# Two transformer blocks on one core: pacing GpSimd's products, and smaller matmul groups in five places

## The chip, the cores and the metric

The kernel runs on one core of a Trainium2 chip. The metric is the device time of one execution in microseconds (us). Three timed runs of the kernel before gave 1594.9, 1595.97 and 1597.15 us (median 1595.97).

A core has five engines, each with an instruction queue of its own that it works off in order: PE (TensorE, matrix products, results into PSUM banks), DVE (VectorE), ACT (ScalarE), POOL (GpSimd, which can't read PSUM) and SP (used here to issue the weight DMAs).

## The reference

256 tokens of width 1024 go through two blocks. All operands are float32.

- The first block: root-mean-square norm; a projection to the inputs of four branches and their gates; a short convolution, stick-breaking attention, an RWKV-7 recurrence and a spatial gating unit (`w_causal` times the normalised `v`, plus a bias `b_s` per group and position, times `u`); the gated sum of the branches, a projection, a residual; then a feed-forward part, `(silu(gate) * val) @ w_down`, with a depthwise convolution of three taps over `h @ w_up` (2 x 2816 columns).
- In the recurrence, `decay = exp(-c * sigmoid(w0 + tanh(xw) @ w2))`, with a bias row `w0` of 256 values.
- The second block: 16 memory tokens are put in front; a state-space branch (S5) with complex diagonal states, an mLSTM branch whose input and forget gates are `concat(q, k, v) @ w_if + b_if`, a gated sum; then a product-key retrieval of experts (128 x 128 experts) and a final norm.

## The kernel before, in words

**Weights.** All weights come as tiles of 128x128; eight of them are a unit, one DMA of 512 KB issued by SP. Each unit is split into a rounded part `wh` (ACT, line 339) and the rest `wl` (DVE, line 340), and each product of float32 accuracy is three matmuls (lines 405 to 407: high times high, high times low, low times high), 24 per unit for 256 tokens. `enter` (line 322) loads up to seven units and splits up to three units ahead, and calls `tick`.

**Background generators.** Work beside the stream of units (the recurrence, the attention, the constants of the S5 branch in `_prep`) is written as Python generators. `tick` (line 366) gives a credit of 1.2 per unit and takes one step of each generator as long as credit is left; a step's yield names its price. `step` and `behind` (lines 348 to 360) put what a step traces on PE, ACT and DVE behind the split and the matmul of some units before, with `tc.issue_after(ins)`: it queues the instructions traced within the block on `ins`'s own engine behind `ins`, in issue order only. On POOL there is no such edge. Apart from these edges and the data, the order of each engine's queue is written by the compiler's planner, which goes by when it expects an instruction's operands.

**The feed-forward loop** (lines 1871 to 1949) has 22 tiles of 128 columns. `up(i)` takes two units (gate and value), 48 matmuls, the convolution on ACT and DVE, silu on ACT, and the gating product `u[:, 0] * u[:, 1]`, which is on POOL for the first 19 tiles (line 1892). The split of a gated tile (ACT's cast, line 429, and DVE's rest, line 430) is traced one tile later, and `down(i - 2)`, 24 matmuls, two tiles later. So three units, 72 matmuls, belong to a tile.

**`_prep`** runs beside that loop from tile 1 on. `paced` (line 559) makes a complex product of 128x512 values as six POOL instructions in four steps (lines 563 to 566). There are eight such products: three of them build the input matrices `bx`, one `c0`, four the output matrices `cx`; then line 583 negates 2048 columns. Beside the last four, eight groups of transposes (line 591) and four groups of small products (line 599) run on PE. Last, eight folds: POOL expands three small matrices (`expand`, lines 490 to 492, called in 635 and 636), PE multiplies each with `w_if` (lines 639 to 641), ACT copies the result.

**Other lines that the change touches.** Lines 1446 to 1451: `tanh(xw) @ w2` on PE, with the bias `w0` added by a product of a row of ones with the row `w0`. Lines 1765 to 1773: eight products of the spatial gating unit into halves of a PSUM bank (64 rows each), each followed by a product of a row of ones with the bias row `sgb`. Lines 839 to 845: the gates of the mLSTM, 16 products that write 8 rows of PSUM each, accumulated in one place. Lines 1276 to 1278: the residual is brought into the four output accumulators by products with the identity, 16 of 128x128. Lines 448 to 457: `rstd` sums squares over the channels with a matrix of ones; it is called after the second projection tile (line 1430), and `K.normed` and the shifts follow from there. Lines 1349 to 1357 issue the first DMAs.

## Time and profile before

| | |
|---|---|
| time, median of three runs | 1595.97 us |
| the profiled execution | 1592.86 us |
| its span | 1591.0 us |
| mean granted TensorE clock | 0.987 |
| busy, share of the span | PE 96%, DVE 72%, ACT 52%, POOL 15% |
| feed-forward loop on PE | 289.3 to 536.1 us |
| read from HBM | 253.23 MB |

The span runs from the first to the last instruction. Busy is the time in which an engine works on an instruction; a busy PE need not run at full clock. In the rows further down, a line of a timeline gives start, duration, engine, line of the kernel and operation, the tile written and those read, the shape and the count of merged instructions; in brackets stands the idle time before it and what ended it. A product of two float32 operands appears as two records, one of the rounded kind as one. A table of stretches gives start and end, length, then for each engine its busy time and its count of instructions, the granted clock as a share of 2.4 GHz, and the DMA engines' share.

### The profile page before, as it was taken

How to read it: one execution, taken by the hardware profiler on the slowest of the kernel's cores; microseconds unless marked ns; L12 is line 12 of the kernel's file. 1: busy time of each engine (PE TensorE's matmuls, PEld its weight loads, DVE VectorE, ACT ScalarE, POOL GpSimd, SP SyncE). 2: the span in 40 equal slices, each digit the busy share in tenths (PEclk: the TensorE clock that was granted, in tenths of full speed). 3: DMA queues.
4: the chain of work that ended last, by engine and by line, in shares of the span. 5: the costliest groups of instructions: out<-in, count | busy, mean ns of one | idle time of the engine just before them, and what ended most of it. 6: DMA issues, size and time to landing. Idle time of an engine off the chain costs nothing.

```text
span 1591.0 us, 29719 instructions
## 1 busy us (share of the span) xinstructions
PE 1535.2 (96%) x11661; PEld 1425.3 (90%) x11661; DVE 1146.4 (72%) x2164; ACT 832.5 (52%) x1439; POOL 237.4 (15%) x254
## 2 busy tenths in 40 slices
PE   7999999987599999999999999999999999999998
PEld 7999899987599997889999999999999888888886
DVE  7765467865477788668899888788999566566664
ACT  7654345744345556555554554544444555555554
POOL 2000000275613002000100431112222000000000
PEclk9999999998899999999999999999999999999999
DMA  7543245544255553245545555555545556556563
GB/s 258 160 136 119 80 133 173 193 146 136 91 174 163 171 166 111 93 134 167 190 159 183 177 158 186 161 161 170 159 160 165 185 194 196 191 195 192 193 197 107
DMA packets 80717, 257.94 MB, mean 162 GB/s; under 512 B 17345, under 2 KB 18881, under 8 KB 80322
## 3 DMA queue, kind: packets, MB, share of 16 engines
q1 hardware_dynamic: 69200, 247.32, 48.3%
q10 hardware_dynamic: 11378, 8.73, 1.9%
q8 instruction: 92, 1.51, 0.4%
q14 instruction: 47, 0.39, 0.1%
HBM read 253.23 MB, written 2.13 MB: 161 GB/s over the span
## 4 chain that ended last, share of the span: by engine, by line
PE 84%; POOL 7%; DVE 6%; ACT 1%; issue 1%; DMA 1%; SPq 0%; ACTq 0%; POOLq 0%; DVEq 0%
PE acc L1297 22%; PE U L405 7%; PE U L407 6%; PE U L406 6%; POOL s L564 4%; PE g L405 3%; PE g L406 3%; PE g L407 3%; DVE wl L340 2%; PE pG L1177 2%; PE u L405 2%; PE u L406 1%; PE u L407 1%; PE q L406 1%; PE q L405 1%; PE q L407 1%
## 5 line engine op out<-in xcount | busy, mean ns | idle before, releaser
L340 DVE TENSOR_TENSOR wl<-wr,wh 128x1024 fp32r<-128x1024 f32 (+1 forms) x469 | 587.4, 1255 | 196.0 <-ACT wh L339 193.1
L339 ACT CAST wh<-wr 128x1024 fp32r<-128x1024 f32 (+1 forms) x469 | 490.6, 1048 | 393.7 <-PE U L406 156.8
L1297 PE MATMUL acc<-wh,wring 128*128 128x512 f32 x1024 | 315.5, 389 | 0.0
L405 PE MATMUL U<-hh,wh 128*128 128x256 f32 x1024 | 292.5, 286 | 0.0
L407 PE MATMUL U<-hh,wl 128*128 128x256 f32 x1024 | 288.1, 281 | 1.5 <-DVE wl L340 1.4
L406 PE MATMUL U<-hl,wh 128*128 128x256 f32 x1024 | 288.3, 282 | 0.0
L1297 PEld LDWEIGHTS acc<-wh,wring 128*128 128x128 f32 x1024 | 192.2, 188 | 40.0
L1297 PE MATMUL acc<-wl,wring 128*128 128x512 f32 x512 | 199.2, 389 | 0.0
L407 PEld LDWEIGHTS U<-hh,wl 128*128 128x128 f32 x1024 | 193.9, 189 | 1.9 <-DVE wl L340 1.9
L405 PEld LDWEIGHTS U<-hh,wh 128*128 128x128 f32 x1024 | 193.4, 189 | 0.0
L406 PEld LDWEIGHTS U<-hl,wh 128*128 128x128 f32 x1024 | 192.5, 188 | 0.0
L1288 ACT ACTIVATE wring<-act 128x256 fp32r<-128x256 f32 x128 | 53.3, 418 | 152.2 <-PE acc L1297 148.7
L1297 PEld LDWEIGHTS acc<-wl,wring 128*128 128x128 f32 x512 | 96.1, 188 | 19.8
L405 PE MATMUL u<-hh,wh 128*128 128x256 f32 x320 | 92.9, 292 | 12.3 <-ACT wh L339 11.6
L1289 DVE SCALAR_TENSOR_TENSOR wring<-act,wring 128x256 fp32r<-128x256 f32 x128 | 54.6, 427 | 60.5 <-PE acc L1297 57.3
L407 PE MATMUL u<-hh,wl 128*128 128x256 f32 x320 | 92.0, 288 | 3.2 <-DVE wl L340 3.2
L406 PE MATMUL u<-hl,wh 128*128 128x256 f32 x320 | 91.4, 287 | 0.0
L1258 POOL TENSOR_TENSOR act<-act,ga 128x16 f32<-128x16 f32 (+31 forms) x77 | 56.5, 733 | 212.4 <-ACT ga L1257 192.3
L444 POOL TENSOR_TENSOR sq<-sq,sq 128x256 f32<-128x256 f32 x18 | 16.0, 888 | 415.4 <-ACT sq L440 415.1
L405 PEld LDWEIGHTS u<-hh,wh 128*128 128x128 f32 x320 | 62.3, 195 | 13.2 <-ACT wh L339 12.0
L405 PE MATMUL g<-hh,wh 128*128 128x256 f32 x256 | 73.8, 288 | 0.0
L406 PE MATMUL g<-hl,wh 128*128 128x256 f32 x256 | 72.0, 281 | 0.0
(643 smaller groups left out, 3411.6 us busy)
## 6 DMA issues: line engine op xcount, KB each, us to landing
wr<-in_W SPq DMA_DIRECT2D x211, 512.0 KB, 3.9
wr<-in_U SPq DMA_DIRECT2D x128, 512.0 KB, 3.9
wr<-in_V SPq DMA_DIRECT2D x128, 512.0 KB, 4.3
s<-in_s5p ACTq DMA_DIRECT2D x1, 1056.0 KB, 6.0
tkc<-in_keysT ACTq DMA_DIRECT2D x1, 1024.0 KB, 6.4
wsA<-in_cst ACTq DMA_DIRECT2D x1, 804.0 KB, 5.2
wsA<-in_rows ACTq DMA_DIRECT2D x1, 640.0 KB, 7.0
s<-s ACTq DMA_DIRECT2D x10, 64.0 KB, 3.0
```

Of the source, the lines that this page charges most:

```text
L339: a = nc.scalar.copy(hi[:, q], raw[:, q])
L340: b = nc.vector.tensor_tensor(lo[:, q], raw[:, q], hi[:, q].bitcast(F32), ALU.subtract)
L405: mm(out, wh, ah, start=first, stop=False)
L406: mm(out, wh, al, start=False, stop=False)
L407: self.last = mm(out, wl, ah, start=False, stop=last).ins
L444: self.nc.gpsimd.tensor_tensor(self.part[0], self.part[0], s, ALU.add)
L564: g.tensor_tensor(*z)
L1177: mm(o, ring[:, q % 2, e // 2, :, e % 2], ring[:, q % 2, 4 + 2 * w + e // 2, :, e % 2], start=w == 0, stop=w == 1)
L1258: g.tensor_tensor(d[:, :n], d[:, :n], a[:, :n], ALU.mult)
L1288: act(hi, w, AF.Copy, scale=1.0 / 16384)
L1289: stt(lo, w, 1.0 / 16384, hi.bitcast(F32), ALU.mult, ALU.subtract)
L1297: mm(acc[t][c], w[:, q], v[:, 4 * c:4 * c + 4].rearrange("p a b -> p (a b)"), start=False, stop=i == NE - 1 and len(vs) == 1, skip_group_c ...
```

## The change

- `up` remembers its gating product (`K.pace`); the block products of `_prep` (six per complex product, the two negations) and the expansions for the folds are traced within `issue_after` of it.
- Each fold's three products are made of halves: rows 0 to 63 and 64 to 127 of the matrices, which are block-diagonal, go into rows 0 to 63 and 64 to 127 of PSUM.
- The 16 products of the mLSTM's gates go in turn to rows 0, 32 and 64 of the bank, that is, to three column groups of PE; the three partial sums are added on ACT and DVE.
- The residual's 16 products with the identity become transposes (`is_transpose=True`).
- The biases `w0` and `sgb` are added on DVE; `sgb` is loaded spread over 128 partitions by two DMAs.
- The start: a tile of zeros is set on POOL, 8 matmuls of zeros with 512 columns are traced before the first DMA, and 3, 6 and 3 more between the first four tiles of the first projection. Only the first 8 columns of `cols` come early, unit 1 of the weights comes before the rest of them and before `eye`. `rstd` is called within the third projection tile, on a bank of the other pool, and the norm and the shifts start one tile later.

```diff
-        self.splits, self.last = [], None
+        self.splits, self.last, self.pace = [], None, None
+    def paced(self):
+
+        return ExitStack() if self.pace is None else self.tc.issue_after(self.pace)
-    def lin(self, seg, i0, kt, hi, lo, out):
+    def lin(self, seg, i0, kt, hi, lo, out, between=None):
         for k in range(kt):
+            if between:
+                between(k)
             wh, wl = self.w(seg, i0 + k)
             self.mm3(out, wh, wl, hi(k), lo(k), k == 0, k == kt - 1)
+    def spin(self, n):
+
+        p = self.pm_("spin")
+        for _ in range(n):
+            self.nc.tensor.matmul(p, self.idle[:, :P], self.idle, start=True, stop=True)
-    def rstd(self):
+    def rstd(self, bank=None):
-        ms = self.ps("ms")[:, :T1]
+        ms = (bank or self.ps)("ms")[:, :T1]
...
         for n, z in enumerate(ops):
-            g.tensor_tensor(*z)
+            with K.paced():
+                g.tensor_tensor(*z)
...
-    g.tensor_scalar(nc0, c0[1], -1.0, None, ALU.mult)
+    with K.paced():
+        g.tensor_scalar(nc0, c0[1], -1.0, None, ALU.mult)
...
-        g.tensor_scalar(cx[1], cx[1], -1.0, None, ALU.mult)
+        with K.paced():
+            g.tensor_scalar(cx[1], cx[1], -1.0, None, ALU.mult)
...
     for e in range(8):
-        for i in range(3):
-            expand(tr[i], e, ex[:, i])
+        with K.paced():
+            for i in range(3):
+                expand(tr[i], e, ex[:, i])
         yield 0.3
         pf = K.ps("pf")
-        mm(pf[:, 0:8], ex[:, 0], wif[:, e], start=True, stop=False)
-        mm(pf[:, 0:8], ex[:, 1], wif[:, 8 + e], start=False, stop=True)
-        mm(pf[:, 8:16], ex[:, 2], wif[:, 16 + e], start=True, stop=True)
+        for i in range(3):
+            for q in (slice(0, 64), slice(64, 128)):
+                mm(pf[q, i // 2 * 8:i // 2 * 8 + 8], ex[q, i, q], wif[q, 8 * i + e], start=i != 1, stop=i != 0)
...
         pg = K.pm_("pg")
-        for e in range(8):
-            mm(pg[:8, :T2], fold[:, 0, e], xc[:, e], start=e == 0, stop=False)
-        for e in range(8):
-            mm(pg[:8, :T2], fold[:, 1, e], xp[:, e, 3:], start=False, stop=e == 7)
+
+        for i in range(16):
+            q = slice(32 * (i % 3), 32 * (i % 3) + 8)
+            mm(pg[q, :T2], fold[:, i // 8, i % 8], (xc[:, i % 8], xp[:, i % 8, 3:])[i // 8], start=i < 3, stop=i > 12)
         act(ga[:8], pg[:8, :T2], AF.Identity, bias=mp[:8, 480:481])
+        for i, z in ((1, gl), (2, gB)):
+            scopy(z[:8], pg[32 * i:32 * i + 8, :T2])
+            tt(ga[:8], ga[:8], z[:8], ALU.add)
...
-            mm(o, xr[:, k, t * P:(t + 1) * P], K.ident, start=k % 4 == 0, stop=False, skip_group_check=True)
+            mm(o, xr[:, k, t * P:(t + 1) * P], K.ident, start=k % 4 == 0, stop=False, is_transpose=True, skip_group_check=True)
...
+    K.idle = K.misc.tile([P, 512], F16, name="idle", tag="ix")
+    nc.gpsimd.memset(K.idle, 0.0)
     act(K.misc.tile([P, 2], F32, name="warm"), eps, AF.Copy)
+    K.spin(8)
     for a, b in ((0, 1), (1, 2), (2, 4), (4, 8)):
         nc.sync.dma_start(xr[:, a:b], I["xT"][:, a:b])
         if a == 0:
-            nc.sync.dma_start(cols, I["cols"])
+            nc.sync.dma_start(cols[:, :8], I["cols"][:, :8])
             K.load(1)
         if a == 1:
             K.piece(1)
+    K.load(2)
+    nc.sync.dma_start(cols[:, 8:], I["cols"][:, 8:])
     nc.sync.dma_start(eye2, I["eye"])
...
-    sgb = C2.a(512)
+
+    sgb = C2.a(2, P)
     with K.behind():
-        nc.scalar.dma_start(sgb[0:1], I["sgb"])
+        for e in range(2):
+            nc.scalar.dma_start(sgb[64 * e:64 * e + 64],
+                                I["sgb"].rearrange("o (c e t) -> o c e t", e=2, t=P)[:, :, e].to_broadcast([64, 2, P]))
...
-        K.lin("rw", j * 8, 8, h0, l0, p[:, :T1])
+        def between(k):
+            nonlocal rs
+            if j == 0 and 0 < k < 4:
+                K.spin((3, 6, 3)[k - 1])
+            if j == 2 and k == 4:
+                rs = K.rstd(K.pm_)
+
+        K.lin("rw", j * 8, 8, h0, l0, p[:, :T1], between)
         wait.append((n, p[:, :T1]))
-        if j == 1:
-            rs = K.rstd()
+        if j == 2:
             nrm = K.start(K.normed(xr, COL["mix_norm_g"], rs, hi1, lo1, T1))
-        if j:
+        if j > 1:
...
-            mm(o, txw[:64, c * P:(c + 1) * P], small[:64, 0:256], start=True, stop=False)
-            mm(o, K.ones[0:1, :], row("rw_w0", 1), start=False, stop=True)
-        act(sg, pL, AF.Tanh, scale=0.5)
+            mm(o, txw[:64, c * P:(c + 1) * P], small[:64, 0:256], start=True, stop=True)
+        tt(sg, pL.rearrange("p (a b) -> p a b", a=2), _bc(row("rw_w0"), 1, 2), ALU.add)
+        act(sg, sg, AF.Tanh, scale=0.5)
...
-                    mm(o, gv[:, t, g * 64:g * 64 + 64], gw[:, g], start=True, stop=False)
-                    mm(o, K.ones[0:1, 0:64], sgb[0:1, g * P:(g + 1) * P], start=False, stop=True)
-        tt(gu, gu, pmx.rearrange("p (a b) -> p a b", a=2), ALU.mult)
+                    mm(o, gv[:, t, g * 64:g * 64 + 64], gw[:, g], start=True, stop=True)
+        four = lambda z: z.rearrange("p c (t b) -> p c t b", t=2)
+        mixed = four(gv)
+        tt(mixed, four(pmx.rearrange("p (a b) -> p a b", a=2)), _bc(sgb, 2, 2), ALU.add)
+        tt(gu, gu, gv, ALU.mult)
...
-        (nc.gpsimd.tensor_tensor if i < NFF - 3 else tt)(u[:, 0], u[:, 0], u[:, 1], ALU.mult)
+        prod = (nc.gpsimd.tensor_tensor if i < NFF - 3 else tt)(u[:, 0], u[:, 0], u[:, 1], ALU.mult)
+        K.pace = prod.ins if i < NFF - 3 else None
```

## Rows read from the trace of the kernel before

**Rows 1.** The page: busy us, share and count of an engine; the chain by engine.
```profile
PE 1535.2 (96%) x11661; PEld 1425.3 (90%) x11661; DVE 1146.4 (72%) x2164; ACT 832.5 (52%) x1439; POOL 237.4 (15%) x254
...
PE 84%; POOL 7%; DVE 6%; ACT 1%; issue 1%; DMA 1%; SPq 0%; ACTq 0%; POOLq 0%; DVEq 0%
```

**Rows 2.** Stretches of the feed-forward loop: PE, PEld, DVE, ACT, POOL, clock, DMA.
```profile
328.00:443.30 115.30, 84.91 (x658) 83.10 (x657) 60.80 (x75) 42.65 (x70) 78.64 (x58) 0.87 0.39 125
455.60:504.50 48.90, 48.90 (x419) 48.90 (x417) 38.62 (x93) 24.73 (x47) 18.38 (x30) 1.00 0.59 180
```

**Rows 3.** Timeline of POOL, 327 to 425 us.
```profile
327.73 1.07 POOL L564 TENSOR_TENSOR s<-s,s 128x512 f32<-128x512 f32 x1
...
335.75 3.90 POOL L564 TENSOR_TENSOR s<-s,s 128x512 f32<-128x512 f32 x2
...
343.11 0.72 POOL L1892 TENSOR_TENSOR ffn<-ffn 128x256 f32<-128x256 f32 x1
...
419.44 5.36 POOL L583 TENSOR_SCALAR s<-s 128x2048 f32<-128x2048 f32 x1
```

**Rows 4.** Waits, 328 to 443 us: us in total, times, longest us.
```profile
ACT ffnr L429 <- POOL ffn L1892: 56.6, 8, 16.6
```

**Rows 5.** Lines 564 and 340 (455 to 504, 328 to 343 us): count, ns min/median/max.
```profile
L564 POOL TENSOR_TENSOR s<-s,s x28: 1043/1051/2035, 323.3 to 417.0; 128x512 f32<-128x512 f32 x28
L564 POOL TENSOR_TENSOR s<-s x20: 1042/1284/2250, 328.9 to 418.1; 128x512 f32<-128x512 f32 x20
...
L340 DVE TENSOR_TENSOR wl<-wr,wh x16: 1209/1222/1737, 460.8 to 502.1; 128x1024 fp32r<-128x1024 f32 x16
...
L340 DVE TENSOR_TENSOR wl<-wr,wh x4: 1214/1874/2299, 328.8 to 336.7; 128x1024 fp32r<-128x1024 f32 x4
```

**Rows 6.** Timeline of PE, 181 to 193 us (attention's values, spatial gating).
```profile
180.98 0.66 PE L1733 MATMUL po<-wsE 128*64 128x256 f32 x4
181.46 0.40 PE L1734 MATMUL po<-wsE 128*64 128x128 f32 x4
...
184.33 0.43 PE L1771 MATMUL pmx<-wsF 128*64 128x128 f32 x2
184.69 0.43 PE L1772 MATMUL pmx<-wsF,eye 1*64 1x128 f32 x2
...
188.29 0.68 PE L1772 MATMUL pmx<-wsF,eye 1*64 1x128 f32 x2
...
191.37 0.58 PE L405 MATMUL br<-ysplit,wh 128*128 128x256 f32 x1
```

**Rows 7.** The stretch 190 to 200 us, columns as in rows 2.
```profile
190.00:200.00 10.00, 10.00 (x61) 8.59 (x61) 5.74 (x9) 2.03 (x3) 0.00 (x0) 0.74 0.05 17
```

**Rows 8.** Timeline of PE at 1232 us (residual) and 237 us (transposes).
```profile
1232.24 3.73 PE L1278 MATMUL acc<-eye,X 128*128 128x128 f32 x32
1235.73 0.47 PE L1297 MATMUL acc<-wh,wring 128*128 128x512 f32 x1
...
237.15 0.60 PE L1676 MATMUL pyt<-eye,wsC 128*128 128x128 f32 x4
237.50 0.36 PE L405 MATMUL g<-hh,wh 128*128 128x256 f32 x1
```

**Rows 9.** Timeline of PE, 624 to 633 us (the mLSTM's gates).
```profile
624.78 3.83 PE L841 MATMUL pg<-ml,s 128*8 128x272 f32 x16
...
632.21 0.38 PE L405 MATMUL g<-hi,wh 128*128 128x256 f32 x1
```

**Rows 10.** Timeline of PE, 41 to 43 us (the decay's bias).
```profile
41.09 0.69 PE L1449 MATMUL pL<-wsA,eye 1*128 1x256 f32 x2
41.72 0.70 PE L1448 MATMUL pL<-wsA,wsB 64*128 64x256 f32 x2
```

**Rows 11.** Timeline of PE, 476 to 477 us (one fold).
```profile
476.40 0.28 PE L639 MATMUL pf<-ml 128*128 128x8 f32 x2
...
476.76 0.37 PE L641 MATMUL pf<-ml 128*128 128x8 f32 x2
```

**Rows 12.** Timeline of PE, 15 to 17 us (the first norm).
```profile
15.97 0.70 PE L453 MATMUL ms<-sq,eye 128*128 128x256 f32 x2 [1.51 <-POOL sq L444]
```

More of the change, by code (lines that the diff above doesn't have):

```diff
@@ L1423, in shift @@
         stt(zp[:, n], zz[:, n, 0:T1], col("rw_mu", n), zp[:, n], ALU.mult, ALU.add)
-    wait = []
+    wait, rs = [], None
     for j, n in enumerate(RW_ORDER):
         p = K.ps("z")
-        K.lin("rw", j * 8, 8, h0, l0, p[:, :T1])
+        def between(k):
[5 more added lines that the diff above has]
+        K.lin("rw", j * 8, 8, h0, l0, p[:, :T1], between)
         wait.append((n, p[:, :T1]))
-        if j == 1:
-            rs = K.rstd()
+        if j == 2:
             nrm = K.start(K.normed(xr, COL["mix_norm_g"], rs, hi1, lo1, T1))
-        if j:
+        if j > 1:
             for w in wait:
```

## The prediction, made before the result was known

> **What bounds the kernel now.** I read the page's busy shares and chain first, then the stretches, then the queue that the worst stretch names. TensorE is busy for 96% of the span, and the chain that ended last runs over it for 84% [rows 1]; but the same row gives 7% to POOL, an engine that is busy for 15%. So most of the kernel gains only from less TensorE work, and somewhere POOL holds TensorE up.
>
> The stretches show where. Undisturbed, the feed-forward part issues 419 matmuls in 48.9 us, 0.1167 us each, at full clock. From 328 to 443.3 us it issues 658 in 115.3 us [rows 2]. At 0.1167 us these are 76.8 us, so 38.5 us are lost there, partly as idle time and partly because the granted clock averages 0.87 of 2.4 GHz, that is, it dropped to the 1.2 GHz level between stalls. POOL is busy for 78.6 of those 115.3 us.
>
> POOL's queue gives the cause: ten block products (L564) stand between 327.73 and 343.11, and only then comes the gating product L1892, which itself takes 0.72 us [rows 3]. ACT's cast of the gated tile waits for it, 56.6 us in eight waits, up to 16.6 us [rows 4], and in ACT's in-order queue the weight casts (L339) stand behind that cast. The second batch ends with the 5.36 us of L583 [rows 3].
>
> **The change, part by part.**
>
> *Block products behind gating products.* Nothing is removed: 48 products (28 of one form, 20 of another [rows 5]) now may issue only behind the last gating product traced. How many stand between two gating products? The background generator makes one step per weight unit; six products are four steps, so 1.5 per unit; a tile of the feed-forward loop has three units (two up, one down), so 4.5 products per tile. Alone they take about 1.05 and 1.28 us [rows 5], so 4.5 cost 5.1 us, and with the gating product (0.72 [rows 3]) POOL needs 5.8 us per tile. TensorE needs 72 x 0.1167 = 8.4 us per tile. The gating product is next due one tile later, when its queue is empty again: the 10 to 16 us waits go, and with them the clock's falls. What is late next? POOL and DVE disturb each other: the weight split L340 takes 1.22 us undisturbed and 1.87 in the first bad stretch [rows 5], and a pair of products takes 3.90 instead of 2.1 us beside it [rows 3, 5]. In those 3.90 us fit 2.1 us of products and, at 1.87 apiece, two splits of 1.22: 4.5 us of work, so only some 15% overlaps. Per tile that is 3 x 1.22 + 5.8 = 9.5 us of both, or 8.1 us with this overlap: just under TensorE's 8.4. The upper bound of the loss is no overlap at all (1.1 us per tile); all 48 products take 48 / 4.5 = 10.7 tiles, so 0 to 12 us. I take 2 us, since the 15% come from this very pair of instructions and the weights are split up to three units ahead. The expansions for the folds are paced too: three POOL instructions per unit, each fold needing those traced a unit before, and behind a gating product that ends after the next down unit has begun. Three gating products fall into these eight steps, so 0 to 3 waits of up to 2.5 us; I take 1.5. Gain: 38.5 - 3.5 = 35 us (bounds 38.5 and 38.5 - 12 - 7.5 = 19).
>
> The Trainium skill, "SBUF — State Buffer", section "Who interferes with whom", says that a DVE instruction with two SBUF inputs and a GpSimd instruction that reads SBUF hold a common port exclusively, the second waiting in full. The trace nearly agrees (4.5 us of work in 3.90). By the rule the loss would be the 12 us, and the total 10 us higher; that outcome is the second rival.
>
> *Spatial biases to VectorE.* From 184.33 to 191.37, 7.04 us, eight products of 128x128 alternate with eight of one row; each pair of records takes 0.36 us, and from 188.29 on 0.6 [rows 6], because the clock fell: granted 0.74 in 190 to 200 us [rows 7]. The one-row half goes. Left are 16 records of 128 columns, 0.109 us each by the 32 of [rows 8] (3.49 us), 1.75 us in series; two column halves side by side are cheaper: four records of 256 columns took 0.48 us from 180.98 to 181.46 [rows 6], against 0.87 at the 0.232 us per 272 columns of [rows 9]. I take 1.5 us, gain 5.5 (bounds 5.3 and 6.0). The 18 or so slow matmuls behind it cost about 0.1 us each more than at full clock; if the clock no longer falls (the engine then does 1.5 instead of 7 us of thin work), 1.6 us more; bounds 0 and 1.6, I take 1.6. The replacing DVE additions are off the path: DVE is busy 5.7 of 10 us there [rows 7], and the block that uses the result comes a branch later. The two small DMAs instead of one cost ACT's queue one more issue, in the start.
>
> *Decay bias to VectorE.* Two pairs of one-row records go, 0.63 us each (41.09 to 41.72 [rows 10]): 1.3 us, bounds 1.0 and 1.3. The DVE addition (half the length of the 1.22 us split, so about 0.7 us) delays only the background chain.
>
> *Memory gates in three column groups.* 32 records take 624.78 to 632.21, 7.43 us, in series [rows 9]. Two halves ran 1.8 times as fast as in series in [rows 6]; three groups at best 3 times. Bounds 7.4 and 2.5 us; I take 2.8, near the best, as all are the same shape: gain 4.6. The two copies and two additions it adds are on 8 partitions, some 1.6 us of the chain; that chain starts 4.6 us sooner, which covers them.
>
> *Residual by transposes.* 32 records, 3.49 us [rows 8], become 16; four transposes take 0.35 us (237.15 to 237.50 [rows 8]), so 16 take 1.4: gain 2.1, bounds 1.7 and 2.1.
>
> *Folds by halves.* Six products of half size for three: twelve records instead of six; a pair now takes 0.28 us, three pairs about 0.6 [rows 11]. Halves may overlap and each turn to another shape may cost; between +3 and -3 us over eight folds, I take 0.
>
> *Start: zeros, earlier unit 1, later norm.* TensorE waited 1.51 us for the squares at 15.97 [rows 12]; moving that product 12 matmuls or more back removes the wait. Against it: 20 products of zeros with 512 columns, 0.47 us or less each at full clock [rows 8], double at half: 9.4 us if none were hidden. But the first eight run before data has landed, and the others in gaps where the first matmuls wait for their inputs. What is late next is the weight splits, which ACT and DVE finish at much the same time as before, since ACT issues the constants' DMAs ahead of them and now one more. The norm's scale comes some 1.4 us later, and what waits for it is DVE. Bounds -4 and +2.5; I take +0.5.
>
> Sum: 35 + 5.5 + 1.6 + 1.3 + 4.6 + 2.1 + 0 + 0.5 = 50.6 us. The profiled execution took 1592.86 us (span 1591.0 and 1.86 around it), which gives 1542.3; it lies 3.1 us under the median of the timed runs, 1595.97, from which the same sum gives **1545**. That is my forecast, with a range of its own of 1536 to 1556.
>
> **The rivals.**
> 1. *Port-bound feed-forward.* POOL and DVE take turns without overlap, gating products come late by a few us all the way, and ACT's cast blocks the weight casts again, in small. For it: products of 1.95 us instead of 1.05 [rows 3]. Against: only while a split runs beside them. Price: 10 us more than I took and 6 of late waits: 1561. It decides from 8.4 us of joint work per tile.
> 2. *Only the pacing pays.* Column groups stay serial, the clock falls in spatial mixing all the same, the zeros cost 4: only 35 + 5.3 + 1.3 + 2.1 - 4 = 40 us: 1556.
> 3. *The pacing doesn't spread.* An edge bounds a product only from below; if the planner still puts ten in a row before a gating product, only the TensorE terms stay, 15.6 us: 1580. Against: the edges allow 4 or 5 behind each.
> 4. *Slower.* TensorE is in order and takes 20 steps that POOL feeds (eight groups of transposes, four of kernel products, eight folds). If POOL's products come late at each because they are held behind gating products, TensorE waits 20 times. From 50.6 / 20 = 2.5 us per step the change loses; at 3 us it is 1605. For it: the fold steps, with a gating product between expansion and use. Against: the transposes' inputs are traced five units, 14 us, before.
>
> **How the numbers follow.** Forecast 0.68, rival 1 0.13, rival 2 0.09, rival 3 0.05, rival 4 0.05. The range 1534 to 1564 takes in rivals 1 and 2 and most of the forecast's own; rivals 3 and 4 and some tails are left out, about 0.18. Differences under 0.2%, 3 us, can't be told from none here. Faster is everything but rival 4 and a small share between: faster 0.93, same 0.02, slower 0.05.
>
> **What would show it.** Pacing: POOL's queue with 4 or 5 block products and then a gating product, ACT's wait for the gating product under 10 us in total, granted clock 1.00 from 328 on, and the feed-forward part about 35 us shorter. Splits near 1.9 us throughout and TensorE waiting for them mean rival 1. Spatial mixing: no one-row matmuls and a block of about 1.5 us, clock 1.00 behind it. Gates: 32 records within 3 us. Residual: 16 records in 1.4 us. Start: no wait for the squares, and the fortieth microsecond reached with about as many matmuls. The prediction is wrong if the feed-forward part gains under 19 us, or if TensorE waits for POOL-fed steps.

## The result, and the profile after

After the change the kernel takes 1555.86 us (median of four runs, 1554.12 to 1556.91), against 1595.43 us for the kernel before on the same chip: a ratio of 0.9751, 95% interval 0.9734 to 0.9768. That is 39.6 us, where 50.6 were forecast; in the profiled spans it is 37.1 us (1591.0 and 1553.9). The sign held, and the forecast's own range of 1536 to 1556 us held by 0.14 us; the size was 11 us too large.

The page after, lines that answer to [rows 1]: busy us with share and count, then the chain by engine.

```profile
PE 1523.9 (98%) x11693; PEld 1416.5 (91%) x11693; DVE 1163.0 (75%) x2168; ACT 832.5 (54%) x1441; POOL 250.5 (16%) x255
...
PE 78%; DVE 11%; POOL 4%; issue 2%; ACT 2%; DMA 1%; SPq 0%; ACTq 0%; DVEq 0%; POOLq 0%
```

POOL does a little more than before and stands for 4% of the chain where it stood for 7. To place the gain I took the start of the first matmul of each part in both traces and noted how far ahead the changed kernel was at that point:

| First matmul of | before, us | after, us | ahead, us | gained in the part before it |
|---|---|---|---|---|
| attention's queries (q) | 37.50 | 36.82 | 0.7 | start 0.7 |
| attention's values (v) | 56.58 | 54.47 | 2.1 | decay bias 1.4 |
| output of the mixers (o) | 266.03 | 256.33 | 9.7 | spatial bias and the clock behind it 7.6 |
| feed-forward (u) | 289.32 | 279.62 | 9.7 | 0 |
| second block (us) | 536.1 | 505.52 | 30.6 | **feed-forward 20.9** |
| its gates (g) | 616.38 | 586.77 | 29.6 | -1.0 |
| next projection (gl) | 704.6 | 669.85 | 34.8 | memory gates 5.2 |
| residual (acc) | 1232.24 | 1197.56 | 34.7 | -0.1 |
| behind the residual | 1235.73 | 1199.23 | 36.5 | residual 1.8 |

These are two single profiles. In the other kernels below, where they leave a part as it is in the changed kernel, the first matmul of q came at 36.0 to 39.3 us, the feed-forward took 224.0 to 228.0 us (225.9 here), and the part behind it 80.3 to 82.8 us. So 0.7 for the start and -1.0 behind the feed-forward mean nothing by themselves, and 20.9 carries some 2 us either way.

The other terms are near what was forecast; the feed-forward gave 20.9 us where 35 stood in the sum. So the question is where 14 us of that one term went.

The products stretch, [rows 2] of before, lies at 318.3 to 433.3 us now. Both its row and the one behind it (columns: busy and count of PE, PEld, DVE, ACT, POOL; granted clock as a share of 2.4 GHz; DMA share; GB/s):

```profile
318.30:433.30 115.00, 111.57 (x935) 110.25 (x933) 98.05 (x121) 55.89 (x92) 96.85 (x62) 1.00 0.55 167
433.30:475.00 41.70, 34.19 (x298) 32.20 (x299) 25.03 (x64) 16.01 (x34) 18.85 (x30) 0.88 0.40 128
```

The stretch that lost 38.5 us now issues 935 matmuls for 658 in the same time, at a clock of 1.00. But a new hole follows: in the 41.7 us behind it TensorE is idle for 7.5 us and the clock averages 0.88. Before the change that work, in its place, ran at 1.00 ([rows 2], second row).

POOL's queue answers to [rows 3] (timeline, start and duration in us):

```profile
324.41 4.02 POOL L577 TENSOR_TENSOR s<-s,s 128x512 f32<-128x512 f32 x2
328.51 1.35 POOL L577 TENSOR_TENSOR s<-s 128x512 f32<-128x512 f32 x1
329.94 3.95 POOL L577 TENSOR_TENSOR s<-s,s 128x512 f32<-128x512 f32 x2
334.04 1.58 POOL L1927 TENSOR_TENSOR ffn<-ffn 128x256 f32<-128x256 f32 x1
...
424.46 6.34 POOL L598 TENSOR_SCALAR s<-s 128x2048 f32<-128x2048 f32 x1
436.03 0.73 POOL L1927 TENSOR_TENSOR ffn<-ffn 128x256 f32<-128x256 f32 x1 [5.22 <-DVE s L566]
436.73 3.69 POOL L504 TENSOR_TENSOR ml<-ml 128x128 f32<-128x128 f32 x6
```

Five products and then a gating product, as the prediction said it would look, and ACT's wait for it ([rows 4]: 56.6 us, longest 16.6) is now

```profile
ACT ffnr L441 <- POOL ffn L1927: 19.8, 10, 3.6
```

The last three rows of POOL show the hole's beginning: the gating product at 436.03 comes late, and the six expansions of the first two folds (L504) stand behind it. The 5.22 us in brackets are POOL's idle time and not the product's lateness. That shows against TensorE: the last up matmul of its tile ended at 427.30, so the product starts 8.73 us behind it, and the next two products start 3.36 and 3.28 us behind theirs. In TensorE's order the first fold stands behind the first half of the next tile, which ended at 433.25, and from there it waits for the expansions (timeline of PE, fold matmuls only):

```profile
438.35 0.39 PE L657 MATMUL pf<-ml 64*64 64x8 f32 x4 [5.10 <-POOL ml L504]
438.99 0.78 PE L657 MATMUL pf<-ml 64*64 64x8 f32 x8 [0.25 <-POOL ml L504]
...
450.89 0.28 PE L657 MATMUL pf<-ml 64*64 64x8 f32 x4 [0.74 <-POOL ml L504]
...
462.98 0.29 PE L657 MATMUL pf<-ml 64*64 64x8 f32 x4 [1.18 <-POOL ml L504]
```

Behind the waits of 5.10 and 1.18 us the matmuls come every 0.21 us for a while instead of every 0.12, the pace of 1.2 GHz instead of 2.4; behind that of 0.74 us they don't (stretches, PE's columns alone: busy, count, granted clock; then the DMA share and GB/s):

```profile
439.70:443.70 4.00, 4.00 (x21) 0.50 0.38 121
451.20:455.20 4.00, 4.00 (x41) 1.00 0.42 135
464.40:467.60 3.20, 3.20 (x17) 0.50 0.30 113
```

### The profile page after: what moved, and what is told of

Same layout as the page of the kernel before. It is cut to its first block, busy times and chain, and to the rows that moved or that the text cites. A ratio compares the mean times of both kernels' runs of the same rounds, so it can differ in the third digit from the quotient of the medians.

```text
span 1553.9 us, 29821 instructions
## 1 busy us (share of the span) xinstructions
PE 1523.9 (98%) x11693; PEld 1416.5 (91%) x11693; DVE 1163.0 (75%) x2168; ACT 832.5 (54%) x1441; POOL 250.5 (16%) x255
## 3 DMA queue, kind: packets, MB, share of 16 engines
q8 instruction: 92, 1.51, 0.4%
## 4 chain that ended last, share of the span: by engine, by line
PE 78%; DVE 11%; POOL 4%; issue 2%; ACT 2%; DMA 1%; SPq 0%; ACTq 0%; DVEq 0%; POOLq 0%
PE acc L1316 22%; PE U L409 6%; PE U L411 6%; PE U L410 6%; DVE wl L340 5%; PE g L409 3%; PE g L411 3%; PE g L410 3%; PE pG L1196 2%; POOL s L577 2%; DVE s L771 1%; PE u L409 1%; PE u L410 1%; PE u L411 1%; ACT wh L339 1%
## 5 line engine op out<-in xcount | busy, mean ns | idle before, releaser
L340 DVE TENSOR_TENSOR wl<-wr,wh 128x1024 fp32r<-128x1024 f32 (+1 forms) x469 | 595.2, 1272 | 199.5 <-ACT wh L339 196.2
L411 PE MATMUL g<-hh,wl 128*128 128x256 f32 x256 | 71.9, 281 | 0.0
```

Of the source, the lines that this page charges most:

```text
L340: b = nc.vector.tensor_tensor(lo[:, q], raw[:, q], hi[:, q].bitcast(F32), ALU.subtract)
L411: self.last = mm(out, wl, ah, start=False, stop=last).ins
```

## Experiments

Three theories stood at the start. One: the tie of the folds' expansions to the gating products is the loss. Two: the 6.34 us negation L598 holds VectorE up (a 128x16 VectorE instruction beside it, L564 at 425.50, took 3.61 us where its kind takes 0.17, first fence below), which makes the gating product late for whoever stands behind it. Three: POOL's traffic slows VectorE's weight splits all along, rival 1 of the prediction.

```profile
425.50 3.61 DVE L564 TENSOR_TENSOR s<-s 128x16 f32<-128x16 f32 x1
429.03 0.16 DVE L565 TENSOR_TENSOR s<-s 128x16 f32<-128x16 f32 x1
```

**Expansions not tied.**

```
     for e in range(8):
-        with K.paced():
+        with ExitStack():
             for i in range(3):
                 expand(tr[i], e, ex[:, i])
```

> The changed kernel, but the 24 expansions of the folds are no longer tied to a gating product; the 49 block products, negations included, still are. Theory 1 (the tie of the expansions is what the feed-forward lost: in the changed kernel TensorE waits 5.10, 0.25, 0.16, 0.74 and 1.18 us ahead of fold matmuls between 438 and 463 us, 7.4 us, and the matmuls of 440 to 470 us run about 6 us slower, at a lower granted clock): most of those 13 us go, 1543 to 1547 us, no wait over 1 us ahead of a fold matmul, granted clock 1.00 between 430 and 470 us. Theory 2 (VectorE is held beside the 6.34 us negation on POOL, so the gating product behind it is late whoever is tied to it): the first fold still waits or the next feed-forward product does; 1553 to 1557 us. Theory 3 (POOL's traffic slows VectorE's weight splits through the whole stretch): 1553 to 1557 us, with the waits spread.

Measured: 1551.77 us (1549.5 to 1553.9), ratio 0.9714 (0.9686 to 0.9743). The feed-forward got 6.2 us shorter (219.7 us from first to first matmul, 225.9 after the change), fold waits fell from 7.4 to 3.9 us, longest 1.9. Less than theory one wanted, more than two or three. The tie is part of it.

**The negation on ScalarE.**

```
-        with K.paced():
-            g.tensor_scalar(cx[1], cx[1], -1.0, None, ALU.mult)
+        for q in range(4):
+            act(cx[1][:, 4 * q:4 * q + 4], cx[1][:, 4 * q:4 * q + 4], AF.Copy, scale=-1.0)
+            if q < 3:
+                yield 0.1
```

> The changed kernel, but the last negation of the output products (one POOL instruction of 6.34 us over 128x2048) is done by ScalarE in four pieces of 128x512; the expansions stay tied. Theory 1: the wait ahead of the first fold stays for the part that is the gating product's own distance; some 2 to 4 us off, 1551 to 1555 us. Theory 2 (VectorE's 3.61 us instruction at 425.5 us beside the negation is the cause): the gating product comes 4 to 5 us earlier, the 5.10 us wait and the clock's fall behind it go; 1543 to 1548 us. Theory 3: 1554 to 1557 us.

Measured: 1556.15 us (1555.11 to 1558.04), ratio 0.9751 (0.9724 to 0.9777): nothing, and by the number only theory three's range holds. The negation does make its product late: that tile's product now starts 5.15 us behind the tile's last up matmul, for 8.73. But the pieces add three steps, so the folds stand some 5 us later behind other gating products; their longest wait fell to 1.23 us, and four waits stay (4.4 us together), with slow matmuls behind them. These products start 5.70, 3.22 and 3.44 us behind their tiles, about as in the changed kernel's tiles without a negation ahead (3.28 to 5.55 us in the six around it). Theory two falls as the account of the loss: a fold tied this closely waits for a product that is on time as well. The run changes two things, the negation's place and the folds' steps.

```profile
445.14 0.66 PE L659 MATMUL pf<-ml 64*64 64x8 f32 x8 [1.14 <-POOL ml L504]
```

**Both.** The two diffs above together.

> The changed kernel with both edits: expansions not tied, the last negation on ScalarE in four pieces. Theory 1: as with free expansions alone, 1542 to 1547 us, within 1.5 us of it. Theory 2: as with the negation on ScalarE alone, 1542 to 1548 us, within 1.5 us of it. If both causes add, it is 3 us or more below either. Theory 3: 1553 to 1557 us.

Measured: 1550.92 us (1548.61 to 1553.02), ratio 0.9712 (0.9684 to 0.974): in none of the three ranges, but within 1 us of the free expansions alone, as theory one wanted.

**No ties at all.** `paced()` returns an empty context always.

> The changed kernel with no block product, negation or expansion tied to a gating product; all its other edits stay. By the first matmuls of the parts, the feed-forward gave 20.9 of the 37.1 us and the rest 16.2. If the two add: 1575 to 1579 us, with TensorE waiting again for gating products between 330 and 445 us. Rival (part of the feed-forward's gain is not the tie but the folds by halves and the earlier start, or the rest leans on the tie): under 1571 us, or over 1583 us.

Measured: 1578.2 us (1576.52 to 1580.01), ratio 0.9882 (0.9854 to 0.991). In the changed kernel all ties together are worth 22.3 us, and the other edits alone 17.2 us of 39.6. That is near the split by first matmuls (20.9 and 16.2), and within what was expected if the two add. The feed-forward is back at 247.9 us (246.8 before), with the old waits in their old places:

```profile
358.59 0.58 PE L409 MATMUL u<-hh,wh 128*128 128x256 f32 x1 [10.07 <-ACT wh L339]
...
418.54 1.12 PE L606 MATMUL pt<-eye,s 128*128 128x128 f32 x4 [13.73 <-ACT s L607]
```

This also disposes of rival 2 of the prediction ("only the pacing pays, 1556"), whose number is the measured one: its mechanism is wrong, since the other edits pay what was forecast and the pacing pays less.

**Expansions two folds ahead, not tied, eight buffers** (with the negation on ScalarE).

```
+    fx = [ZZ.t[:, 384 * e:384 * e + 384].rearrange("p (a b) -> p a b", a=3) for e in range(8)]
+    def expansions(e):
+        for i in range(3):
+            expand(tr[i], e, fx[e][:, i])
+    expansions(0)
+    expansions(1)
+    yield 0.3
     for e in range(8):
+        if e < 6:
+            expansions(e + 2)
         yield 0.3
...
-                mm(pf[q, i // 2 * 8:i // 2 * 8 + 8], ex[q, i, q], wif[q, 8 * i + e], start=i != 1, stop=i != 0)
+                mm(pf[q, i // 2 * 8:i // 2 * 8 + 8], fx[e][q, i, q], wif[q, 8 * i + e], start=i != 1, stop=i != 0)
```

> The changed kernel with the last negation on ScalarE in four pieces, and the folds' expansions not tied, written two folds ahead of their matmuls into a buffer of their own for each of the eight folds, so that no expansion waits for TensorE to read the last one. Theory A (what is left of the fold waits after both edits, 0.66 and 0.90 us ahead of a matmul and some 3 us of slow matmuls behind the second, comes from the single buffer): no wait ahead of a fold matmul over 0.3 us, granted clock 1.00 from 430 to 490 us, the feed-forward 213 to 216 us long by the first matmuls of its parts (217.3 with both edits, 225.9 in the changed kernel), 1546 to 1550 us. Theory B (the expansions come late because POOL or the gating products are late, not for the buffer): the waits stay, 1550 to 1553 us. Theory C (what is saved here is given back behind later waits, where the clock falls or not by chance): the feed-forward shortens as in A, the time stays at 1550 to 1553 us.

Measured: 1547.4 us (1546.27 to 1547.85), ratio 0.9685 (0.9666 to 0.9705), the fastest whole kernel here and clear of the changed kernel's interval. No fold waits; the feed-forward is 216.4 us. Two new waits show what a free expansion costs: with nothing to hold it, it can issue as soon as its table is there, here some 70 us early, between two block products, and five of them delay a gating product:

```profile
372.11 1.82 POOL L504 TENSOR_TENSOR s<-ml 128x128 f32<-128x128 f32 x5
373.89 0.72 POOL L1937 TENSOR_TENSOR ffn<-ffn 128x256 f32<-128x256 f32 x1
```

```profile
376.62 0.63 PE L608 MATMUL pt<-eye,s 128*128 128x128 f32 x4 [3.55 <-ACT s L609]
...
453.58 0.36 PE L409 MATMUL u<-hh,wh 128*128 128x256 f32 x1 [2.30 <-DVE ffn L1935]
```

The first rows are POOL's timeline, the second PE's, both of this run; the first of the two waits was 1.10 us in the changed kernel.

**Output products cut to an eighth.** The 24 output products and their negation work on 2 of 16 column groups; this leaves out seven eighths of the second state-space product's output matrices, which are zero there.

```
-            yield from paced(qr, qi, pr, pi_, bar, bai)
+            yield from paced(qr, qi, pr, pi_, bar, bai, 2)
...
-            g.tensor_scalar(cx[1], cx[1], -1.0, None, ALU.mult)
+            g.tensor_scalar(cx[1][:, 0:2], cx[1][:, 0:2], -1.0, None, ALU.mult)
...
+    for z in cx:
+        g.memset(z, 0.0)
```

> The changed kernel, but the 24 output products and their negation work on an eighth of their columns (128x64 for 128x512, 128x256 for 128x2048); the rest of the output matrices is zero, and so the second state-space product is left out for these. Same instructions, ties and order; POOL's traffic in 365 to 431 us falls by about seven eighths. Theory 1 (contention between POOL and VectorE is the smaller part): the waits at 365.85, 377.78 and 419.07 us (2.3 us together) go, VectorE's weight splits in 365 to 431 us fall from 1.45 to about 1.25 us, the fold wait of 5.10 us shrinks to 1 to 3 us since VectorE is not held beside the negation; 1548 to 1553 us. Theory 2 (contention is most of the shortfall): 1540 to 1546 us.

Measured: 1545.23 us (1544.04 to 1549.42), ratio 0.967 (0.9651 to 0.969). The groups of VectorE from 365 to 431 us, of the changed kernel and then of this one (count, busy us, mean ns, idle ahead):

```profile
L340 DVE TENSOR_TENSOR wl<-wr,wh 128x1024 fp32r<-128x1024 f32 x18 | 30.7, 1718 | 2.5 <-ACT wh L339 2.4
```

```profile
L340 DVE TENSOR_TENSOR wl<-wr,wh 128x1024 fp32r<-128x1024 f32 x20 | 25.7, 1288 | 9.6 <-ACT wh L339 9.4
```

So the products lengthen each weight split by a third (1718 for 1288 ns) and double the rest of the gated tile's split (L442, 910 for 465 ns on the mean). But what TensorE loses by it between 365 and 431 us is small: three waits go (1.10, 0.52 and 1.09 us, 2.7 together), one of 0.7 stays. The feed-forward is 9.8 us shorter (216.1 us); most of the other 7 lies at the folds, which come 8 us sooner and whose longest wait is 1.19 us for 5.10; the product behind the short negation starts 3.87 us behind its tile, for 8.73. By its waits theory 1 of this run is right, but for the wait of 0.7 us that it expected to go; its time, 1548 to 1553, was too cautious by 3 us, and the number alone would have spoken for theory 2.

**The spatial bias as before**, in one-row matmuls (the three hunks of the change on `sgb` undone).

> The changed kernel with the spatial gate's bias as it was before, in sixteen one-row matmuls instead of VectorE; everything else as changed. By the first matmuls of the parts this edit gave 7.6 us where 5.5 were forecast (7.1 with the clock). If that reading holds: 1562 to 1565 us. Rival (the part got shorter for another reason, the clock there or the order of the work around): 1556 to 1560 us.

Measured: 1564.16 us (1563.15 to 1565.34), ratio 0.9791 (0.9771 to 0.9811): 8.3 us more, the reading by first matmuls (7.6) holds: in its profile the same part is 7.6 us longer again (209.5 us from v to o, 201.9 in the changed kernel).

**The memory gates in one column group** (the hunk on `pg` undone, with the copies and additions behind it).

> The changed kernel with the memory gates' sixteen matmuls in one column group as before, without the two copies and two adds behind them. The first matmuls of the parts give this edit 5.2 us, 4.6 were forecast: 1560 to 1562 us. Rival (the three groups only move the wait, and the clock makes the rest): 1555 to 1558 us.

Measured: 1564.79 us (1563.78 to 1565.77), ratio 0.9797 (0.9777 to 0.9817): 8.9 us more, above the expected 4 to 6. The block itself is back at 7.43 us (3.06 in the changed kernel); behind it the clock falls as told of in the last section (granted clock 0.90 from 655 to 675 us here). From the second block's gates to the last projection its profile takes 218.6 us, where the kernel before, with the same gates, takes 213.9: 4.6 us for that fall. Together that is 9.0; in its profile the feed-forward, whose code is the same, happened to be 1.9 us shorter.

**Without the matmuls of zeros** (both calls of `spin` left out).

> The changed kernel without the matmuls of zeros (the 8 ahead of the first product and the 12 within its first column); the other edits of the start stay. The forecast gave the whole start 0.5 us, bounds -4 to +2.5, the first matmuls of the parts 0.7. If the matmuls of zeros give that by the clock: 1556 to 1558 us, matmuls of the first columns at 0.21 us steps until 14 us as before the change, the third column released by the same weight splits at the same time within 1 us. Rival (the other edits of the start carry it, or the third column waits for the weights either way): 1554.5 to 1556 us.

Measured: 1555.96 us (1555.55 to 1557.51), ratio 0.9755 (0.9738 to 0.9771): no difference. The zeros do raise the clock: matmuls of the first column come every 0.12 us from 9.6 us on with them and from 11.8 us on without. Then both wait for the same weights, and the third column starts 0.1 us apart. PE of the changed kernel, then of this one:

```profile
18.26 0.38 PE L409 MATMUL z<-h,wh 128*128 128x256 f32 x1 [0.94 <-ACT wh L339]
```

```profile
18.16 0.39 PE L409 MATMUL z<-h,wh 128*128 128x256 f32 x1 [0.94 <-ACT wh L339]
```

**Expansions tied, but three folds ahead.** As the lead of two, with the tie kept and the negation on POOL.

```
+    for e in range(11):
+        if e < 8:
+            with K.paced():
+                for i in range(3):
+                    expand(tr[i], e, fx[e][:, i])
+        yield 0.3
+        e -= 3
+        if e < 0:
+            continue
```

> The changed kernel with the folds' expansions still tied to the gating products, but written three folds ahead of their matmuls, into a buffer of their own for each fold; the last negation stays on POOL. Theory A (the matmuls of a fold stand too close behind expansions that sit behind a gating product): waits ahead of fold matmuls under 1 us together, granted clock 1.00 behind them, 10 to 13 us less in the feed-forward, 1543 to 1547 us. Theory B (VectorE held beside the 6.34 us negation is the cause): the next feed-forward product waits in the fold's place, 1549 to 1554 us.

Measured: 1548.91 us (1547.03 to 1550.75), ratio 0.9712 (0.9695 to 0.9728). The gating product is as late as ever, 8.72 us behind its tile's last up matmul, and no fold waits for it any more:

```profile
425.42 6.35 POOL L598 TENSOR_SCALAR s<-s 128x2048 f32<-128x2048 f32 x1
436.99 0.76 POOL L1932 TENSOR_TENSOR ffn<-ffn 128x256 f32<-128x256 f32 x1 [5.22 <-DVE s L566]
```

```profile
442.70 0.52 PE L662 MATMUL pf<-ml,s 64*64 64x8 f32 x12
444.82 0.36 PE L409 MATMUL u<-hh,wh 128*128 128x256 f32 x1 [1.60 <-DVE ffn L1930]
```

The feed-forward is 215.7 us, 10.2 less, so theory A holds and theory B of this run falls: what takes the fold's place waits 1.60 us. The time misses the expected 1547 by 2 us, because 3 us are lost again behind it (last section).

**The same with the negation on ScalarE.**

> As the run before it, with the last negation on ScalarE in four pieces besides. Theory A: within 2 us of that run, 1542 to 1547 us, no wait like the 3.55 us at 376 us of the untied lead of two, since no expansion gets ahead of a gating product. Theory B: 3 us or more below that run.

Measured: 1554.45 us (1553.54 to 1556.05), ratio 0.9749 (0.9733 to 0.9765): a miss on both theories. The pieces of the negation and the lead add three steps each, and the last six folds stand behind all 38 up units of the 19 tiles on POOL, where by the code `K.finish(prep)` takes all steps that are left at once. Three folds' matmuls issue together at 457.31. The next three wait, since their expansions are tied behind the last of POOL's gating products, at 460.87, and only four matmuls of the feed-forward stand between the two groups.

```profile
460.87 1.57 POOL L1934 TENSOR_TENSOR ffn<-ffn 128x256 f32<-128x256 f32 x1 [2.74 <-DVE ffn L1932]
462.40 3.43 POOL L504 TENSOR_TENSOR s<-ml 128x128 f32<-128x128 f32 x9
```

```profile
457.31 1.39 PE L664 MATMUL pf<-ml,s 64*64 64x8 f32 x36
462.85 0.74 PE L664 MATMUL pf<-ml,s 64*64 64x8 f32 x8 [2.63 <-POOL s L504]
```

A lead of a fixed number of steps thus helps only as long as the steps are taken one per unit; where the rest of a generator is taken at once, there is no lead left.

**The kernel before with the block products tied, and nothing else.**

```
-            g.tensor_tensor(*z)
+            with K.paced():
+                g.tensor_tensor(*z)
...
+        K.pace = prod.ins if i < NFF - 3 else None
```

> The kernel before, with its 49 block products (the two negations among them) tied to the gating products and nothing else of the change; the folds' expansions stay untied and whole. In the changed kernel all ties together were worth 22.4 us (1578.2 without any), and untying the expansions alone gave 4.1 back. If the ties act alone: 26 us off, 1567 to 1572 us, the feed-forward some 27 us shorter by the first matmuls of its parts (246.75 before). Rival (the folds by halves or the other edits carry part of it, or the untied expansions get ahead of a gating product): 20 us off or less, 1575 us or more.

Measured: 1564.55 us (1563.82 to 1564.69), ratio 0.981 (0.9791 to 0.9829): 29.9 us off, past the expected 26 and the range. Its feed-forward is 215.9 us, 30.9 less than before, and the clock stays at 1.00 through the folds. The feed-forward stretches, first to first matmul, of before, after, the tied lead and this kernel, one fence each (columns as above):

```profile
289.30:536.10 246.80, 214.54 (x1737) 211.43 (x1735) 163.87 (x298) 122.90 (x204) 109.53 (x102) 0.94 0.47 150
```

```profile
279.60:505.50 225.90, 213.20 (x1784) 208.66 (x1783) 180.36 (x298) 122.43 (x204) 123.98 (x102) 0.98 0.52 164
```

```profile
280.50:496.20 215.70, 208.87 (x1784) 205.52 (x1783) 180.98 (x298) 122.15 (x204) 122.91 (x102) 0.99 0.55 171
```

```profile
291.30:507.20 215.90, 208.70 (x1736) 205.82 (x1735) 181.18 (x298) 122.21 (x204) 123.01 (x102) 1.00 0.53 172
```

Length less PE's busy time is its idle time: 32.3, 12.7, 6.8 and 7.2 us. Two ways of freeing the fold matmuls from the late gating product, one with the folds by halves and one with whole folds, end at the same 216 us. The nearer pair is less even: with free expansions the folds by halves gave 219.7 us in the first run and whole folds give 215.9 here. The first run has a second fold wait, 1.90 us, with 13 matmuls at 0.21 us behind it, this one only the first (1.68 and 0.25 us) and none at 0.21. In the times it is the same: 29.9 us for these ties and 17.2 for the other edits would make 47.1, and the first run was some 44 below the kernel before.

## Why the prediction was right, and where it was not

*Feed-forward, forecast 35 us, measured 20.9.* The step that failed is the sentence on the folds: "0 to 3 waits of up to 2.5 us; I take 1.5". Tying the expansions without a lead cost 10.2 us (225.9, against 215.7 with a lead of three), with some 2 us of play. Of it 5.9 us are idle time (12.7 less 6.8), 1.6 are 17 more feed-forward matmuls at 0.21 us (32 and 15), and the rest I put down to folds that issue in pieces, not counted one by one: the first takes 1.34 us, where a whole one takes 0.45. Three folds waited, as many as I allowed for, and 7.4 us in all are just within the 7.5 that bounded them. What I had wrong is the 1.5: I priced only a gating product that is on time, not one that starts 8.73 us behind its tile, and nothing for the clock behind the waits. By the prediction's last sign, "if TensorE waits for POOL-fed steps", it was wrong here, though the total stayed in its range. Rival 4 described this mechanism and named the fold steps as what speaks for it, but I kept it as an all-or-nothing case of 20 waits, where three folds waited.

The products' own part is 30.9 us by the kernel with these ties alone, where 36.5 (38.5 less 2) stood in the prediction. Of these 5.6 us, 1.4 are the waits at 365.85, 373.32, 377.78 and 419.07 us (0.67, 1.10, 0.52 and 1.09, together 3.4) against 2 for the disturbance between POOL and VectorE; 1.9 are waits of folds in that kernel; and some 1.7 were never to be had, since 0.1167 us a matmul was low for this stretch: 935 matmuls now take 111.57 us of busy time at a clock of 1.00, 0.1193 each, which makes 78.5 us for 658 and not 76.8. The disturbance itself is as large as in the pair that I read (3.90 us a pair, splits of 1.87): a pair of products took up to 4.02 us, and splits 1.72 us on the mean. But most of it hides behind weights that are split ahead, as was argued.

The Trainium skill, "SBUF — State Buffer", section "Who interferes with whom", has a VectorE instruction with two SBUF inputs and a POOL instruction that reads SBUF hold their shared port exclusively. Durations here agree in part: the 128x16 VectorE instruction that took 3.61 us began inside a POOL instruction of 6.34, but ended at 429.11, 1.69 us before that one did. Rival 1, which the prediction also calls the second, rested on this and priced it at 16 us through TensorE; the products stretch shows 3.4 us of waits, so the exclusion, as far as it holds, does not reach TensorE at that price.

*Spatial bias, 5.5 and 1.6 forecast, 7.6 measured; 8.3 by undoing it.* The block is now shorter than the 1.5 us I took, and the clock behind it stays at 1.00, so [rows 7]'s 0.74 is gone:

```profile
182.22 1.15 PE L1804 MATMUL pmx<-wsF 128*64 128x128 f32 x16
183.29 0.39 PE L409 MATMUL br<-ysplit,wh 128*128 128x256 f32 x1
```

```profile
188.00:198.00 10.00, 10.00 (x99) 9.12 (x100) 7.92 (x14) 3.41 (x6) 0.00 (x0) 1.00 0.31 107
```

The first fence is PE's timeline, the second the stretch behind it.

*Decay bias:* 1.3 and 1.4 (17.65 us from q to v for 19.08, though the kernel before with ties alone took 20.58 there). *Memory gates:* 4.6 and 5.2; the block takes 3.06 us, from 594.96 to 598.02, for the 2.8 that I took, and one wait of 1.41 us for VectorE is new in the part behind it. It is no price of this edit: the kernels with the gates in one group, but with ties, have it too, and the two without ties don't. *Residual:* 2.1 and 1.8, sixteen transposes in 1.67 us:

```profile
1197.56 1.91 PE L1297 MATMUL acc<-eye,X 128*128 128x128 f32 x16
1199.23 0.47 PE L1316 MATMUL acc<-wh,wring 128*128 128x512 f32 x1
```

*Folds by halves:* 0 forecast; six pairs take 0.52 us. No effect is shown: 215.7 and 215.9 us speak for none, 219.7 and 215.9 for a cost of up to 4 us, which is as much as the feed-forward differs between kernels with the same code there (last section). *Start:* 0.5 and 0.7, but nothing is shown: q comes at 36.0 to 39.3 us in the eleven profiles with the changed start, at 37.5 and 37.9 with the old one. The wait for the squares fell from 1.51 to 0.15 us, and waits of 0.94 and 0.45 us for the weight casts are new behind it.

ACT's wait for the gating product was to fall under 10 us and is 19.8; its longest is 3.6 us, and in that stretch TensorE has no wait of 0.3 us or more for a weight cast. With 20.9 in place of 35 the sum of 50.6 becomes 36.5, and the spans give 37.1.

## What to carry to other kernels

An instruction tied behind another takes over that one's lateness, and so does whatever an in-order engine does next with its result: before tying a step, look for how far its consumer stands behind it, and give it a lead. Here three steps, one tile of the loop, were enough while the steps came one per unit, and not where they were taken at once; a longer lead was not tried. Price such a wait with what follows it: here the idle time was 5.9 of 10.2 us. Read lateness against the work that feeds a step, not by the idle time in front of it, which is also the time in which an engine has nothing to do. And a total can match a rival's number for the wrong reason; the first instruction of each part, before and after, tells which term was off before any experiment is made.

## What was not expected of the hardware

The same wait is followed by different clocks. At 666.5 us the changed kernel has a wait of 1.41 us (pN for VectorE), and the tied lead of three has the same one at 656.2. In the changed kernel the matmuls behind it run at 2.4 GHz, in the tied lead of three at 1.2 GHz for several us. Stretches, PE's columns alone (busy, count, granted clock), the changed kernel first:

```profile
665.00:670.00 5.00, 3.59 (x14) 1.00 0.24 65
670.00:675.00 5.00, 5.00 (x40) 1.00 0.77 247
```

```profile
652.00:657.00 5.00, 3.59 (x27) 1.00 0.00 0
657.00:662.00 5.00, 5.00 (x12) 0.54 0.53 175
662.00:667.00 5.00, 5.00 (x32) 0.77 0.75 245
```

From the first matmul of the second block's gates to that of the last projection (U) it costs 3.0 us: 211.8 us in the tied lead, 208.8 in the changed kernel. The profiles with free expansions, alone (211.8) and with the negation on ScalarE (212.0), and both with the tied lead of three (211.8 and 211.7) show it. With the outputs cut (213.4) and with the gates in one group (218.6, for 213.9 in the kernel before) it costs 4.6. Those with the negation alone, the free lead of two, without zeros, with the spatial bias undone, and of the kernel before with ties have the wait and no fall.

The feed-forward shows the same. Four kernels have the changed kernel's code there and its waits of 5.1 and 1.2 us ahead of folds. But the matmuls at 0.21 us are 22 with the gates in one group, 32 in the changed kernel, 48 without zeros and 49 with the spatial bias undone, and the part takes 224.0, 225.9, 228.0 and 227.8 us. With the gates in one group the wait of 1.19 us at 462.81 is followed by a clock of 1.00, where the changed kernel had 0.50 behind its 1.18:

```profile
464.00:467.20 3.20, 3.20 (x35) 1.00 0.37 146
```

It differs between executions of one kernel too: the profiled one with the outputs cut took 1549.42 us, the three others 1544.04 to 1545.55. With one profile of each kernel I can't say what decides; it stays open, and a gain upstream of such a place can't be counted to better than these 3 to 5 us.

Small matmuls on separate column groups overlap well: 32 gate matmuls with 272 columns took 3.06 us in three groups against 7.43 in one, 2.4 times as fast, and sixteen of 128x128 in two halves 1.07 us, against 3.49 for 32 in series, 1.6 times.
